# Hybrid SSD and forgetting-attention layer: the stores of the output weights' differences, issued by GpSimd instead of the load queue

## The chip, the cores and the metric

The kernel runs on one core of one Trainium2 chip. A core has five engines that run side by side, each with its own queue in order: TensorE (PE in the profile; PEld is its weight load), VectorE (DVE), ScalarE (ACT), GpSimd (POOL) and SyncE (SP), which here only issues DMAs. An engine whose next instruction must wait on a semaphore stops there, and all that stands behind it waits too. A DMA is issued by an engine (SP, ScalarE or GpSimd here) and then moves its bytes on the core's 16 DMA engines. The metric is the device time of one execution in microseconds (us).

## The reference

A decoder layer for 1024 positions of width 1024, in float32, with two branches beside each other:

```python
h    = _rmsnorm(x, pre_g)
proj = jnp.einsum('bld,de->ble', h, w_in)   # z_ssm xBC dt | q k v f | z_att g_ssm g_att
...                                          # xBC: causal convolution of 4 taps, silu
y    = _ssd_chunked(xs, dt, a, b_ssm, c_ssm, d_skip)      # 8 chunks of 128 positions, 16 heads of 64
y_ssm = grouped_rmsnorm(y * silu(z_ssm)) * ssm_norm_g
o     = _forgetting_attention(q, k, v, log_f)             # softmax(q k' / 8 + F[t] - F[s]), causal
y_att = o * silu(z_att)
p_ssm = jnp.einsum('ble,ed->bld', y_ssm, w_branch_ssm)
p_att = jnp.einsum('ble,ed->bld', y_att, w_branch_att)
merged = sigmoid(g_ssm) * p_ssm + sigmoid(g_att) * p_att
out   = jnp.einsum('bld,de->ble', merged, w_out)
x     = x + _rmsnorm(out, post_g)
```

(shortened: `grouped_rmsnorm` stands for the four groups' norm that the reference writes out). The part that the change touches prepares `w_out`, the 1024 x 1024 output weights, for the last product.

## The kernel before

**Products with fewer multiplications.** Every large product is done on 2 x 2 blocks with seven block products instead of eight (class `Pair`). The moving operand is a matrix of four blocks b11, b12, b21, b22; beside blocks themselves the seven products need four differences of them: t1 = b12 - b11, t2 = b22 - t1, t3 = t2 - b11, t4 = t2 - b21. Each block product is twelve matmuls of 512 columns into one PSUM bank: four steps of 128 rows, each with high and low parts of the operands (high x high, high x low, low x high), since a float32 value is split into a rounded part and its remainder. The stream of products (class `Stream`) advances by half steps of six matmuls, `Stream.half`.

**Stages.** The stream of projections runs from the start to the end. Beside it run, in turn: a prologue that normalises and transposes x; for four groups of heads the convolution, the chunked recurrence (`ssd`) and the gated norm; then attention for eight pairs of heads; last the two branch products, the merge and the output product. A generator of the other work yields how many half steps of the stream go between its own pieces.

**The output weights' differences.** In the last product the output weights are the moving operand; the object `ops_w` of class `Operands` (line 1182) stands for it. Its differences are made early, during the stage of the recurrence. `weights_work` (L1054) makes a list of chores, for 4 row blocks and 2 halves of 256 columns, eight pieces in all, and `Stream.half` takes one chore per half step (L1353 hands them over). The chores of one piece come from `differences` (L200) with `room` 4, which is the number of empty chores between a load and its use:

- load b12 into tile x (L230) and b11 into tile y (`fetch`, L209), both from SP;
- four empty chores; GpSimd subtracts t1 = x - y into x (L214); then `keep`: store t1 (L196) and load b22 into y;
- four empty chores; the low part of b22 by ScalarE and VectorE (L240, L241) and its store from SP (L248); GpSimd subtracts t2 = y - x into x; `keep`: store t2 and load b11 into y;
- four empty chores; t3 = x - y into y, `keep`: store t3; its low part (L243, L244) and store (L248); three empty chores; load b21 into y; four empty chores;
- t4 = x - y into x; `keep`: store t4; low part and its store.

Each x and y is a single tile of 128 x 256 float32, one pair for each half; the tile of the low part, `wl`, is a single one. The stores go to a DRAM copy and are read back for the last product, after 1100 us. So 32 subtractions, 32 stores of differences (L196), 24 stores of low parts (L248) and 40 loads.

**Order.** `pin` keeps an instruction in program order within its engine. The subtractions, the stores and the low parts' roundings are pinned, and `ops_w` is made with `order=pin`, which pins its loads, and `queue=nc.sync`, so that its stores go by SP. The other two operands, `ops_s` and `ops_a`, have the default queue, GpSimd. All that isn't pinned is ordered at build time by a planner with its own estimate of times, which also sets the semaphore waits.

**Neighbours on the queues.** In the same stage SP issues the projections' weight loads (`raw`, L348), the loads and stores of the recurrence (csb L861, z L996, ys L1051), and stores of q, k, v and z (L672, L688, L689, L845). GpSimd does three steps for each chunk of the recurrence: `xe` (L906) that feeds the state's product, `ce` (L913) that feeds the output's, and the decay of the state `new` (L927), to which VectorE adds the chunk's part (L931). The copy of a product out of PSUM on ScalarE is L412, the split of the stationary operand L355 (ScalarE) and L357 (VectorE), its sums L364 and L380.

## Time and profile before

| | |
|---|---|
| median of 3 runs | 1288.71 us (1287.9 to 1292.36) |
| profiled execution | 1288.07 us; span of its instructions 1286.4 us |
| granted TensorE clock, mean | 0.998 |
| busy in the span: TensorE, VectorE, ScalarE, GpSimd | 1248.9, 1016.0, 797.3, 288.5 us |
| DMA: moved, mean rate | 233.60 MB, 182 GB/s |
| queue of SP (q1), GpSimd (q0), ScalarE (q10): share of the DMA engines | 49.6%, 3.4%, 2.2% |

The span runs from the first to the last instruction of the profiled execution; its own time is 1.67 us longer. In the views, L196 is line 196 of the kernel; a `q` behind an engine's name is its sequencer, which waits, branches or issues; "idle before" is how long an engine did nothing before an instruction, and the arrow names whose semaphore ended that. `wd` is the name of both tiles x and y, `t_w` of the DRAM copies of the differences, `wl` of the low part's tile. A matmul's record is longer than the step from one matmul to the next, since they overlap.

### The profile page before, as it was taken

How to read it: one execution, taken by the hardware profiler on the slowest of the kernel's cores; microseconds unless marked ns; L12 is line 12 of the kernel's file. 1: busy time of each engine (PE TensorE's matmuls, PEld its weight loads, DVE VectorE, ACT ScalarE, POOL GpSimd, SP SyncE). 2: the span in 40 equal slices, each digit the busy share in tenths (PEclk: the TensorE clock that was granted, in tenths of full speed). 3: DMA queues.
4: the chain of work that ended last, by engine and by line, in shares of the span. 5: the costliest groups of instructions: out<-in, count | busy, mean ns of one | idle time of the engine just before them, and what ended most of it. 6: DMA issues, size and time to landing. Idle time of an engine off the chain costs nothing.

```text
span 1286.4 us, 21104 instructions
## 1 busy us (share of the span) xinstructions
PE 1248.9 (97%) x7066; PEld 986.9 (77%) x7066; DVE 1016.0 (79%) x1979; ACT 797.3 (62%) x1728; POOL 288.5 (22%) x307
## 2 busy tenths in 40 slices
PE   6999999999999999899999999999999999999998
PEld 4787888788887888778777777777777777678886
DVE  6998888798789888788677766766678877976976
ACT  8745666566556656566556666666667655753754
POOL 0000330024102320043001222222111222346052
PEclk9999999999999999999999999999999999999999
DMA  7333543545353454445475664666678657766933
GB/s 282 98 110 70 159 143 126 194 142 153 129 192 124 149 170 150 136 140 144 162 243 173 215 221 161 235 208 209 202 276 269 212 194 241 238 203 201 372 114 101
DMA packets 154669, 233.60 MB, mean 182 GB/s; under 512 B 17216, under 2 KB 62656, under 8 KB 154560
## 3 DMA queue, kind: packets, MB, share of 16 engines
q1 hardware_dynamic: 142016, 205.53, 49.6%
q0 software_dynamic: 6400, 16.10, 3.4%
q10 hardware_dynamic: 6144, 10.62, 2.2%
q8 instruction: 56, 0.92, 0.3%
q14 instruction: 53, 0.43, 0.1%
HBM read 162.99 MB, written 72.34 MB: 183 GB/s over the span
## 4 chain that ended last, share of the span: by engine, by line
PE 70%; DVE 11%; DMA 9%; ACT 5%; issue 4%; SPq 1%; POOL 1%; DVEq 0%; ACTq 0%
PE pb L130 30%; PE pc L130 17%; PE pd L130 5%; PE av L130 4%; PE pt L133 4%; PE s L130 4%; DVE wop L357 2%; PE yps L130 2%; DMA raw<-in_wu 2%; DMA q<-qh_dram 1%; PE tr L133 1%; PE st L130 1%; DMA xt<-in_x 1%; ACT wop L355 1%; DVE sum L364 1%
## 5 line engine op out<-in xcount | busy, mean ns | idle before, releaser
L357 DVE TENSOR_TENSOR wop<-sum,wop 128x512 fp32r<-128x512 f32 x174 | 138.1, 794 | 58.1 <-ACT wop L355 56.6
L355 ACT ACTIVATE wop<-sum 128x512 fp32r<-128x512 f32 x174 | 108.8, 626 | 99.0 <-DVE sum L364 45.1
L1563 ACT ACTIVATE ex<-ex,nm 128x512 f32<-128x512 f32 (+1 forms) x192 | 116.0, 605 | 55.4 <-DVE nm L1558 55.0
L412 ACT ACTIVATE s<-pb 128x512 f32<-128x512 f32 x141 | 83.6, 593 | 103.0 <-PE pb L130 89.1
L357 DVE TENSOR_TENSOR wop<-raw,wop 128x512 fp32r<-128x512 f32 x149 | 114.2, 768 | 37.0 <-ACT wop L355 36.9
L130 PE MATMUL pc<-x3h,wop 128*128 128x512 f32 x384 | 132.3, 401 | 2.6 <-ACT wop L355 2.0
L130 PE MATMUL pb<-x0h,wop 128*128 128x512 f32 x384 | 132.5, 401 | 0.1
L130 PE MATMUL pc<-x2h,wop 128*128 128x512 f32 x384 | 131.9, 400 | 0.3 <-DVE u L424 0.3
L130 PE MATMUL pb<-x5h,wop 128*128 128x512 f32 x376 | 127.9, 397 | 2.2 <-ACT s L412 2.2
L130 PE MATMUL pb<-x6h,wop 128*128 128x512 f32 x376 | 128.3, 397 | 1.3 <-ACT s L412 1.3
L130 PE MATMUL pb<-x4h,wop 128*128 128x512 f32 x376 | 127.6, 397 | 0.3 <-DVE wop L357 0.3
L1558 DVE CUSTOM_DVE_ANT_0 ex<-s,fb 128x512 f32<-128x512 f32 (+1 forms) x192 | 96.4, 551 | 12.7 <-PE s L130 12.7
L355 ACT ACTIVATE wop<-raw 128x512 fp32r<-128x512 f32 x151 | 94.0, 624 | 19.0 <-PE pc L130 11.3
L130 PE MATMUL pd<-x1h,wop 128*128 128x512 f32 x264 | 89.1, 395 | 0.0
L130 PEld LDWEIGHTS pc<-x3h,wop 128*128 128x128 f32 x384 | 72.8, 190 | 20.7 <-ACT wop L355 3.7
L130 PEld LDWEIGHTS pc<-x2h,wop 128*128 128x128 f32 x384 | 72.1, 188 | 17.1 <-issue 1.5
L130 PEld LDWEIGHTS pb<-x0h,wop 128*128 128x128 f32 x384 | 72.6, 189 | 16.4 <-issue 0.6
L130 PEld LDWEIGHTS pb<-x5h,wop 128*128 128x128 f32 x376 | 70.7, 188 | 18.4 <-ACT s L412 3.0
L130 PEld LDWEIGHTS pb<-x6h,wop 128*128 128x128 f32 x376 | 70.6, 188 | 16.9 <-ACT s L412 1.7
L130 PEld LDWEIGHTS pb<-x4h,wop 128*128 128x128 f32 x376 | 70.5, 188 | 16.2 <-DVE wop L357 0.9
L214 POOL TENSOR_TENSOR wd<-wd 128x256 f32<-128x256 f32 x32 | 30.4, 951 | 228.4 <-DMA wd<-in_wo 108.2
L130 PE MATMUL pc<-x3l,wop 128*128 128x512 f32 x192 | 75.7, 394 | 0.7 <-DVE x3l L282 0.7
(342 smaller groups left out, 3002.6 us busy)
## 6 DMA issues: line engine op xcount, KB each, us to landing
raw<-in_wu SPq DMA_DIRECT2D x128, 256.0 KB, 3.9
csb<-cs_dram SPq DMA_DIRECT2D x32, 256.0 KB, 5.5
fb<-f_dram SPq DMA_DIRECT2D x16, 512.0 KB, 6.2
wd<-in_wo SPq DMA_DIRECT2D x40, 128.0 KB, 3.3
rb<-st_dram SPq DMA_DIRECT2D x34, 128.0 KB, 3.2
xt<-in_x SPq DMA_DIRECT2D x8, 512.0 KB, 5.8
gs_dram<-th ACTq DMA_DIRECT2D x16, 256.0 KB, 3.6
qh_dram<-th SPq DMA_DIRECT2D x16, 256.0 KB, 4.2
```

What stands on the lines that cost most here:

```text
L130: return tc.keep_in_program_order(nc.tensor.matmul(*args, **kw))
L133: return tc.keep_in_program_order(nc.tensor.transpose(out_, in_, idn))
L214: pin(nc.gpsimd.tensor_tensor(t[out_], t[a_], t[b_], ALU.subtract))
L355: nc.scalar.activation(op[:, 0], src, AF.Copy, scale=sign)
L357: nc.vector.tensor_tensor(op[:, 1], src, op[:, 0], ALU.subtract)
L364: self.adds.tensor_tensor(t, x, y, ALU.add)
L412: nc.scalar.activation(s, ps, AF.Copy)
L1558: nc.vector.tensor_tensor_reduce(to, bank(u, e), fb[hp, h][:, e, 0 : w[u]], 1.0, 3.0e38, ALU.add, ALU.min, nm)
L1563: nc.scalar.activation(to, to, AF.Exp, scale=-1.0, bias=nm, accum_out=hd.at(hd.sm, i, h, e))
```

## The change

The method `store` of `Operands`, which writes a difference to DRAM, no longer issues its DMA from the queue that the object was made with but always from GpSimd. For `ops_s` and `ops_a` that is the same queue as before; for `ops_w` the 32 stores of 128 x 256 values move from SP's queue to GpSimd's. The stores of the low parts at L248 use the object's queue still, so they stay on SP.

```diff
         def store(self, name, j, t, cols=slice(0, HALF)):
-            pin(self.queue.dma_start(self.dram[name][j][:, cols], t))
+            pin(nc.gpsimd.dma_start(self.dram[name][j][:, cols], t))
             if cols.stop == HALF:
                 self.made.add((name, j))
```

On GpSimd the store takes the place in program order that it had: in the chore behind the subtraction's, with whatever GpSimd does for the recurrence in between.

## Prediction

> **What bounds the kernel now.** I read the page first, then the busy times by stretch, then the waits of TensorE, and only then the queue that the change touches.

> ```profile
> span 1286.4 us, 21104 instructions
> PE 1248.9 (97%) x7066; PEld 986.9 (77%) x7066; DVE 1016.0 (79%) x1979; ACT 797.3 (62%) x1728; POOL 288.5 (22%) x307
> 127.00:645.00 518.00, 511.60 (x2680) 412.96 (x2679) 429.58 (x715) 319.66 (x646) 115.78 (x112) 1.00 0.48 151
> ```

> The last row gives the length, the busy time of TensorE, its weight loads, VectorE, ScalarE and POOL, the granted clock and the DMA's share for the stretch from the first load of the output weights (127.9 us) to the last piece of their differences. TensorE is idle for 518.0 - 511.6 = 6.4 us in it. POOL works 115.8 us of 518, so it has room; SP's queue only matters through what it delivers late to others. Whatever the change takes off a queue can win no more than those 6.4 us and what they cause. TensorE's waits in the same stretch name their causes:

> ```profile
> PE pc L130 <- ACT wop L355: 2.0, 1, 2.0
> PE pb L130 <- ACT s L412: 1.3, 1, 1.3
> PE st L130 <- POOL xe L906: 1.2, 2, 0.9
> PE tr L133 <- DVE xs L813: 1.1, 1, 1.1
> ```

> There are few stalls and each is short. The sum below asks which of them the stores stand behind.

> **The change part by part.** It moves 32 stores of 128 KB (t1 to t4, eight pieces each). The 24 stores of low parts at L248 stay on SP, and so do the 40 loads.

> ```profile
> L209 SPq DMA_DIRECT2D wd<-in_wo x32: 333/423/737, 128.3 to 625.6; - x32
> L214 POOL TENSOR_TENSOR wd<-wd x32: 725/742/1954, 133.3 to 628.5; 128x256 f32<-128x256 f32 x32
> L196 SPq DMA_DIRECT2D t_w<-wd x32: 319/382/609, 135.2 to 638.0; - x32
> SPq L196 <- POOL wd L214: 25.1, 11, 4.2
> ```

> *Removed from SP:* 32 x 0.382 = 12.2 us of issuing, and 25.1 us in 11 waits for the subtraction, by these rows. Only part of the waiting goes. After t1 and t2 the very next entry is the load of the next block into y, and y is read by the same subtraction, so that load must wait for it just as the store did; the wait moves from L196 to L209. After t3 and t4 the next entry of that chain is the low part's store, which waits for VectorE's rounding that itself follows the subtraction; other transfers may slip in before it. So what surely remains is the issue time of one store, with its step to the next (0.42 us, from 525.30 to 525.72 in the chain below), by which the following load leaves earlier.

> *What those 0.42 us are worth.* The longest stall, 2.0 us, hangs on such a load. The chain of waits there:

> ```profile
> 524.03 1.25 POOL wd L214
> 525.30 0.33 SPq L196
> 525.72 3.27 DMA wd<-in_wo
> 529.07 0.04 ACT wl L240
> 529.40 0.58 ACT s L412
> 530.53 0.70 DVE wop L357
> 534.46 0.69 DVE sum L364
> 535.23 0.56 ACT wop L355
> 535.88 0.47 PE L130 MATMUL pc<-x3h,wop 128*128 128x512 f32 x1 [2.04 <-ACT wop L355]
> ```

> The subtraction ends at 525.28, SP issues the store, then the load of b22 at 525.72; it lands at 528.99, and ScalarE, which works in order, is stopped at the rounding L240 until then. Behind it stand the copy out of PSUM (L412) and the weights' split, then VectorE's queue, and TensorE starts 2.04 us late. Without the store the load leaves at about 525.30 and everything behind it moves up 0.42 us. That is **-0.4 us**.

> *The clock behind that stall.* Granted clock around this stall, and around the 1.3 us stall at 250.18:

> ```profile
> 537.00:540.00 3.00, 3.00 (x9) 2.32 (x8) 3.00 (x6) 2.31 (x8) 0.00 (x0) 0.50 0.51 157
> 248.00:252.00 4.00, 2.71 (x12) 1.90 (x12) 2.29 (x5) 1.42 (x3) 0.73 (x1) 1.00 0.77 250
> ```

> After 2.04 us of idle TensorE ran at half clock for some 3 us and 9 matmuls, so about 1.5 us were lost besides; after 1.3 us it did not. With the stall cut to 1.6 us it lies between the two, a little nearer to 1.3. A dip that stays is worth 0, one that goes 1.5 us; I take **-0.8** and keep both ends. [...]

> *Other loads on SP* behind one of the 32 stores also leave up to 0.4 us earlier, but TensorE's other stalls in the list are held by something else: the 1.3 us one by a b21 load that SP issued right behind a store waiting for VectorE, the 1.1 us one by VectorE's convolution. Bounds: 0 to the rest of the 6.4 us (4.4); value 0, as no row links them to a store.

> *Added on POOL.* The trace has no store of 128 KB from POOL; the nearest are those of the same line for the other operands, 256 KB.

> ```profile
> L196 POOL DMA_DIRECT2D t_s<-x x12: 547/577/600, 691.9 to 894.2; - x12
> 696.00 0.59 POOL L196 DMA_DIRECT2D t_s<-x  x1 [0.31 <-POOL x L214]
> DMA to landing us min/median/max: 2.4/5.0/6.8
> ```

> Each takes 0.58 us of POOL, and 0.31 us more where it stands directly behind its subtraction. So 32 x (0.58 to 0.89) = 18.6 to 28.5 us on an engine that is idle for 402 us of the stretch. Behind it on POOL stand the recurrence's own steps:

> ```profile
> 149.83 0.74 POOL L214 TENSOR_TENSOR wd<-wd 128x256 f32<-128x256 f32 x1
> 150.53 1.15 POOL L927 TENSOR_TENSOR new<-new,cdec 128x256 f32<-128x256 f32 x1
> 154.48 0.61 POOL L906 TENSOR_TENSOR xe<-xdt,tend 128x256 f32<-128x256 f32 x1 [2.80 <-DVE xdt L874]
> POOL xe L906 <- DVE xdt L874: 199.4, 28, 70.5
> 159.27 0.39 PE L130 MATMUL yps<-ce,new 128*64 128x128 f32 x4
> ```

> In the worst order the store sits between 149.83's subtraction and the state's decay `new`, which then starts 0.89 us later, at about 151.4. The state is read by the second `yps` after it, at 159.27, so some 7 us cover it. The next step, `xe`, waits for VectorE: all 28 do, (199.4 - 70.5) / 27 = 4.8 us each without the first, 2.80 us in this row, which swallows 0.89. Cost **0**; if the cover were gone, at most one store before each of the 28 steps, 28 x 0.89 = 24.9 us, is the upper bound. VectorE's addition behind `new` can be 0.9 us late in some places; VectorE is idle 88 us of the stretch.

> *The data's way.* The differences are read back only after 1100 us; the landing time plays no part there. Within a piece, t2 overwrites the tile that t1's store reads, so t2 waits for that landing: the second rival.

> **Sum.** 1288.07 us (this execution: span 1286.4 and 1.67 around it) - 0.4 - 0.8 + 0 = 1286.9. This execution was 0.64 us under the median of the runs (1288.71), so I forecast 1287.5 for the median, within 0.1% of before.

> **The rivals.**

> *SP was worth more.* Both waits at t3 and t4 and the earlier loads remove the 2.0 and 1.3 us stalls, the clock dip, and 1.2 to 2.5 us more. Time: 1288.7 - (2.0 + 1.3 + 1.5 + 1.2) = 1282.7. For it: 25.1 us of waiting at the head of the queue. Against: y ties the next load to the same subtraction.

> *The store's landing becomes the wait (slower).* Now t2 follows t1 closely where SP had fallen behind:

> ```profile
> 205.60 0.33 SPq L196 DMA_DIRECT2D t_w<-wd  x1
> 208.58 0.74 POOL L214 TENSOR_TENSOR wd<-wd 128x256 f32<-128x256 f32 x1 [3.01 <-DMA wd<-in_wo]
> ...
> 529.15 0.74 POOL L214 TENSOR_TENSOR wd<-wd 128x256 f32<-128x256 f32 x1 [3.88 <-DMA wd<-in_wo]
> t_w<-wd SPq DMA_DIRECT2D x32, 128.0 KB, 3.2
> ```

> From SP a store lands in 3.2 us. From POOL, with the 5.0 us of the 256 KB stores, issued at 205.9, it lands at 210.9 and t2 starts 2.3 us later (4.1 with 6.8). Four pieces look like this, the first and the last of them shown. If t3's rounding on ScalarE followed t2 at once, ScalarE would stop 2.3 us four times and TensorE with it: 1288.7 + 9.2 = 1297.9, and up to four clock dips of 1.5 us more. It decides only once the lateness exceeds the room between t2 and t3, which the program sets at six half steps of six matmuls, at least 6 x 6 x 0.227 = 8.2 us (0.227 us is TensorE's step, as from 528.41 to 528.64 in the timeline). 2.3 and 4.1 both stay below it.

> ```profile
> 528.41 0.39 PE L130 MATMUL pd<-x1l,wop 128*128 128x512 f32 x1
> 528.64 0.61 PE L130 MATMUL pd<-x1h,wop 128*128 128x512 f32 x2
> ```

> *POOL's stores stretch beside VectorE.* POOL's arithmetic does stretch here; beside it the busy times of the rest of the program:

> ```profile
> L906 POOL TENSOR_TENSOR xe<-xdt,tend x28: 612/614/3003, 132.7 to 593.8; 128x256 f32<-128x256 f32 x28
> ```

> ```profile
> 645.00:1287.00 642.00, 622.15 (x3850) 485.43 (x3848) 477.94 (x1057) 394.78 (x928) 171.53 (x187) 1.00 0.64 214
> ```

> If a store took 3.0 us as the longest `xe` did, 0.3 + 3.0 = 3.3 would exceed the 2.80 us before `xe` by 0.5; with a store before half of the 28 steps that is 7 us: 1295.7. Against it: the stores of the later stages took 547 to 600 ns while VectorE was busy 478 of 642 us, 74%, against 83% here. [...]

> *The planner orders the rest anew.* Only pinned instructions keep program order; others are ordered at build time by estimated times, which the move changes. The largest event seen costs 2.0 + 1.5 = 3.5 us, so one more or one fewer gives 1285.2 to 1292.2.

> *Nothing moves:* the wait simply passes to L209 and the 0.42 us are lost elsewhere: 1288.7.

> **How the numbers follow.** Forecast 0.55, SP worth more 0.12, landing 0.07, stretched stores 0.03, planner 0.16, nothing moves 0.07. A measurement of this kernel can tell about 0.5% from no change, 6.4 us: below 1282.3 or above 1295.2. Below: half of the first rival (0.06) and 0.02 of the planner's; above: 0.09 from landing, stretching and the planner's tail. The forecast's own range is 1286 to 1289 (dip gone or kept, and 0.5 of scatter); for 8 in 10 it reaches into the first rival and the planner's ends, 1283.5 to 1292.5.

> **What would show it.** Right: no L196 on SP; POOL's stores at 0.55 to 0.60 us and most behind their subtraction by 0.3; L209's waits for POOL growing by part of the 25.1 us; TensorE's idle time in the stretch 5 to 7 us; the stall at 535.88 at 1.6 us. Wrong: POOL stores of 1 us or more, `st` or `yps` waiting for POOL in many places, t2 waiting for the store's landing with ScalarE stopped at L243 behind it, or new stalls in the attention stage, which would be the planner's.

## The result, and the profile after

The changed kernel takes 1297.88 us (median of 6 runs, 1294.80 to 1301.76), against 1290.12 us for the kernel before beside it (6 runs, 1287.78 to 1292.36): ratio 1.0062, 95% interval [1.0044, 1.0080]. It is slower by 0.6%, outside the range that was forecast (1283.5 to 1292.5). Its profiled execution took 1296.72 us with a span of 1294.9 us, 8.5 us longer than that of before.

The page of the changed kernel, and the stretch of the output weights' pieces in the columns of the prediction (length, busy time of TensorE, its weight loads, VectorE, ScalarE and GpSimd, granted clock, DMA share, GB/s):

```profile
span 1294.9 us, 21110 instructions
PE 1248.9 (96%) x7066; PEld 986.5 (76%) x7066; DVE 1016.3 (78%) x1979; ACT 797.0 (62%) x1728; POOL 304.6 (24%) x339
127.00:645.00 518.00, 506.01 (x2657) 408.69 (x2655) 423.47 (x705) 316.51 (x642) 134.44 (x144) 1.00 0.48 148
```

TensorE has exactly the work of before, 1248.9 us. In the stretch its idle time rose from 6.4 to 518.0 - 506.0 = 12.0 us. Its waits there name the causes (us in total, times, longest):

```profile
PE yps L130 <- DVE m L884: 3.4, 2, 1.7
PE pb L130 <- ACT s L412: 2.7, 1, 2.7
PE tr L133 <- DVE xs L813: 2.1, 1, 2.1
PE pc L130 <- ACT wop L355: 1.4, 1, 1.4
PE pc L130 <- DVE u L424: 1.3, 2, 0.8
PE st L130 <- POOL xe L906: 0.9, 1, 0.9
```

The first line is new: before, `yps` waited for nobody. The second grew from 1.3 to 2.7 us, the fourth shrank from 2.0 to 1.4. The operations that were moved look as they were forecast; this is the group view of `wd`, and the waits of SP in the stretch:

```profile
L214 POOL TENSOR_TENSOR wd<-wd x32: 719/830/1930, 133.2 to 633.8; 128x256 f32<-128x256 f32 x32
L196 POOL DMA_DIRECT2D t_w<-wd x32: 557/559/762, 135.4 to 634.8; - x32
SPq L209 <- POOL wd L214: 7.7, 5, 2.5
```

A store costs GpSimd 0.56 us, SP has none left, and of its 25.1 us of waiting for the subtraction 7.7 us stayed, now at the loads.

Matching the two traces matmul by matmul shows where the 8.5 us arise. The stop near 250 us is 1.4 us longer, and half clock behind it costs 1.6 more. The two waits for `m`, near 291 and 431 us, add 1.7 and 1.9, two waits near 394 and 550 us 0.8 each. The stop that the prediction counted on, at 535.88, gives back 2.1 with its half clock. With small steps between that makes 5.7 us at 557 us; 2.8 more come behind 645 us, 1.6 of them in one place near 1113 us.

The orders of the two programs explain part of it. Engine by engine, compared by line and tile: SP, ScalarE, GpSimd and TensorE have the same order in both but for the 32 moved stores, VectorE has seven exchanges, that is, pairs of instructions whose order is turned round. So the planner did order anew, on one engine. What the seven exchanges cost and what the stores cost had to be parted by experiment.

### The profile page after: what moved, and what is told of

Its sections match the earlier page's. It is cut to its first block, busy times and chain, and to the rows that moved or that the text cites. A ratio compares the mean times of both kernels' runs of the same rounds, so it can differ in the third digit from the quotient of the medians.

```text
span 1294.9 us, 21110 instructions
## 1 busy us (share of the span) xinstructions
PE 1248.9 (96%) x7066; PEld 986.5 (76%) x7066; DVE 1016.3 (78%) x1979; ACT 797.0 (62%) x1728; POOL 304.6 (24%) x339
## 4 chain that ended last, share of the span: by engine, by line
PE 69%; DVE 11%; DMA 9%; ACT 5%; issue 4%; SPq 1%; POOL 0%; DVEq 0%; ACTq 0%; POOLq 0%
PE pb L130 31%; PE pc L130 16%; PE pd L130 5%; PE av L130 4%; PE pt L133 4%; PE s L130 4%; DVE wop L357 3%; PE yps L130 2%; DMA raw<-in_wu 2%; DMA wd<-in_wo 1%; PE tr L133 1%; DMA xt<-in_x 1%; DVE sum L364 1%; PE st L130 1%; DMA th<-gs_dram 1%
## 5 line engine op out<-in xcount | busy, mean ns | idle before, releaser
L357 DVE TENSOR_TENSOR wop<-sum,wop 128x512 fp32r<-128x512 f32 x174 | 138.5, 797 | 56.9 <-ACT wop L355 56.5
L355 ACT ACTIVATE wop<-sum 128x512 fp32r<-128x512 f32 x174 | 108.8, 626 | 99.0 <-DVE sum L364 45.4
L412 ACT ACTIVATE s<-pb 128x512 f32<-128x512 f32 x141 | 83.7, 594 | 105.6 <-PE pb L130 91.7
L357 DVE TENSOR_TENSOR wop<-raw,wop 128x512 fp32r<-128x512 f32 x149 | 115.8, 779 | 37.6 <-ACT wop L355 37.4
L130 PE MATMUL pc<-x3h,wop 128*128 128x512 f32 x384 | 131.2, 398 | 2.4 <-ACT wop L355 1.4
L130 PE MATMUL pc<-x2h,wop 128*128 128x512 f32 x384 | 132.0, 400 | 1.3 <-DVE u L424 1.3
L130 PE MATMUL pb<-x0h,wop 128*128 128x512 f32 x384 | 132.2, 400 | 0.4 <-ACT x0h L1253 0.3
L130 PE MATMUL pb<-x6h,wop 128*128 128x512 f32 x376 | 129.4, 400 | 2.7 <-ACT s L412 2.7
L130 PE MATMUL pb<-x5h,wop 128*128 128x512 f32 x376 | 128.0, 397 | 2.8 <-ACT s L412 2.8
L130 PE MATMUL pb<-x4h,wop 128*128 128x512 f32 x376 | 127.6, 397 | 0.3 <-DVE wop L357 0.3
L355 ACT ACTIVATE wop<-raw 128x512 fp32r<-128x512 f32 x151 | 94.0, 624 | 19.0 <-PE pc L130 11.3
L130 PE MATMUL pd<-x1h,wop 128*128 128x512 f32 x264 | 89.1, 395 | 0.0
L130 PEld LDWEIGHTS pc<-x3h,wop 128*128 128x128 f32 x384 | 72.1, 188 | 20.1 <-issue 2.8
L130 PEld LDWEIGHTS pc<-x2h,wop 128*128 128x128 f32 x384 | 72.2, 188 | 18.5 <-DVE u L424 2.2
L130 PEld LDWEIGHTS pb<-x6h,wop 128*128 128x128 f32 x376 | 71.3, 190 | 18.6 <-ACT s L412 3.2
L130 PEld LDWEIGHTS pb<-x0h,wop 128*128 128x128 f32 x384 | 72.6, 189 | 16.8 <-ACT x0h L1253 1.1
L130 PEld LDWEIGHTS pb<-x5h,wop 128*128 128x128 f32 x376 | 70.6, 188 | 19.4 <-ACT s L412 4.1
L130 PEld LDWEIGHTS pb<-x4h,wop 128*128 128x128 f32 x376 | 70.5, 188 | 16.0 <-issue 0.7
L214 POOL TENSOR_TENSOR wd<-wd 128x256 f32<-128x256 f32 x32 | 31.8, 994 | 213.9 <-DMA wd<-in_wo 161.5
L1465 POOL DMA_DIRECT2D st_dram<-st x48 | 27.3, 571 | 210.8 <-ACT st L1463 207.7
## 6 DMA issues: line engine op xcount, KB each, us to landing
wd<-in_wo SPq DMA_DIRECT2D x40, 128.0 KB, 3.0
rb<-st_dram SPq DMA_DIRECT2D x34, 128.0 KB, 3.1
```

The costliest lines, as they stand in the source:

```text
L130: return tc.keep_in_program_order(nc.tensor.matmul(*args, **kw))
L214: pin(nc.gpsimd.tensor_tensor(t[out_], t[a_], t[b_], ALU.subtract))
L355: nc.scalar.activation(op[:, 0], src, AF.Copy, scale=sign)
L357: nc.vector.tensor_tensor(op[:, 1], src, op[:, 0], ALU.subtract)
L412: nc.scalar.activation(s, ps, AF.Copy)
L1465: pin(nc.gpsimd.dma_start(st_dram[self.hp, n, :, 256 * h : 256 * h + 256], st[4 * h : 4 * h + 4, :]))
```

## The experiments

All ratios are to the kernel before, run beside them. The last column is the mean over all runs of the granted clock; what half clock costs is estimated as (1 - clock) x span: 3.6 us for before (0.9972), 5.8 for the changed kernel (0.9955).

| run | median us | ratio, 95% interval | clock |
|---|---|---|---|
| changed kernel | 1297.88 | 1.0062 [1.0044, 1.0080] | 0.9955 |
| e4, the same again | 1296.11 | 1.0049 [1.0032, 1.0066] | 0.9950 |
| e2, VectorE's new order alone | 1296.52 | 1.0044 [1.0027, 1.0062] | 0.9958 |
| e13, two of its exchanges alone | 1294.99 | 1.0040 [1.0025, 1.0056] | 0.9963 |
| e3, changed, these two undone | 1292.25 | 1.0015 [1.0001, 1.0030] | 0.9952 |
| e1, 32 stores on GpSimd, order of before | 1293.57 | 1.0022 [1.0004, 1.0039] | 0.9956 |
| e14, the same again | 1293.74 | 1.0034 [1.0021, 1.0046] | 0.9952 |
| e6, 31 stores | 1291.70 | 1.0006 [0.9992, 1.0020] | 0.9958 |
| e5, one store | 1290.46 | 1.0001 [0.9988, 1.0014] | 0.9970 |
| e9, the first 20 stores | 1288.60 | 0.9987 [0.9972, 1.0001] | 0.9968 |
| e10, the last 20 stores | 1288.24 | 0.9984 [0.9972, 0.9997] | 0.9978 |
| e7, early load of b21, stores on SP | 1289.89 | 0.9995 [0.9984, 1.0007] | 0.9968 |
| e8, the same, 32 stores on GpSimd | 1293.16 | 1.0024 [1.0013, 1.0035] | 0.9956 |
| e12, early load for the output weights alone | 1287.60 | 0.9979 [0.9962, 0.9997] | 0.9980 |
| e15, the same with the last 20 stores | 1285.25 | 0.9963 [0.9948, 0.9978] | 0.9985 |

e11 ran once, in 1292.76 us, and so has no ratio. Lines in these kernels lie up to 20 further on than in before, since names were added: m L884 is L900 or L902 there.

### The order and the stores, each alone

An ordering edge tells the planner which of two instructions of an engine comes first; it adds no wait. Numbers count each kind in program order.

```diff
+    def queue_behind(later, earlier):     # (kind, number): later stands behind earlier
+        tc.add_manual_dep(marks[later].ins, marks[earlier].ins.name, NoSync)
...
 # e1: changed kernel, every engine in the order of before
+    queue_behind(wop 40, new 1); queue_behind(z 7, new 6); queue_behind(z 11, new 12)
+    queue_behind(sum 33, m 10); queue_behind(sum 51, m 18)
+    queue_behind(xdt 11, sum 34); queue_behind(xdt 27, sum 70); queue_behind(xdt 3, sum 16)
 # e2: kernel before, VectorE in the order of the changed kernel
+    queue_behind(new 1, wop 40); queue_behind(new 6, z 7); queue_behind(new 12, z 11)
+    queue_behind(m 10, sum 33); queue_behind(m 18, sum 51)
+    queue_behind(sum 34, xdt 11); queue_behind(sum 70, xdt 27)
 # e3: changed kernel;  e13: kernel before, with the two the other way round
+    queue_behind(sum 33, m 10); queue_behind(sum 51, m 18)
```

(The expectation of e1 speaks of nine edges; there are eight.) e4 has no edit.

> The changed kernel with nine ordering edges, so that every engine's order of instructions is the one of before; what is left of the change is that GpSimd issues the 32 stores. Theory 'order' (all of the 7.8 us come from VectorE's new order): within 1.5 us of the kernel before, about 1290, and TensorE's waits for VectorE's m L884 (1.65 and 1.73 us) gone. Rival 'stores' (the two waits for m are the order's, 3.5 us, the rest is from the stores on GpSimd: the later landing of the b21 load at 243 us, its clock dip, the drift behind 645 us): 3 to 5 us slower than before, about 1294, with a stop of TensorE of 2.7 us near 250 and half clock behind it. The prediction's own sum (-0.4 and -0.8): 1 us faster than before.

> The kernel before, its stores still on SP, with seven ordering edges that give VectorE the order of the changed kernel; all other engines keep theirs. Theory 'order': as slow as the changed kernel, 6 to 9 us over before, about 1298, with two waits of TensorE's yps for m L884 near 290 and 431 us. Rival 'stores': only the two waits, 3.5 us over before, about 1293.6.

> The changed kernel with two edges only: the sums L364 that wait for a raw load go behind the decay product m L884 again, in the second chunk of groups 1 and 2; the other exchanges of VectorE's order stay. If the two waits cost what TensorE's idle time shows: 3.5 us faster than the changed kernel, about 1294.4. If the time goes elsewhere behind the two waits (given back later): under 1.5 us faster. If the clock or later stages hang on them as well: 6 us or more faster.

> The changed kernel once more, unaltered: a second profile. If the longer landing of the b21 load at 243 us (6.63 us) and the half clock at 253 us belong to the kernel, they are there again, with TensorE's stop of 2.7 us near 250; if they are chance of one execution, the stop is 1.3 us as before and the profile is some 2.8 us shorter. Time 1297.9 within 2 us.

> The kernel before, stores on SP, and two ordering edges alone: in the second chunk of groups 1 and 2 the sum L364 that waits for a raw load goes ahead of the decay product m L884. If the whole loss of VectorE's new order is these two: 4 to 6 us slower than before, ratio 1.003 to 1.0045, two waits of TensorE's yps for m L884 of 1.7 us or more. If the five other exchanges carry a part: ratio under 1.0025.

The order alone costs 0.44%, 5.7 us, with the stores still on SP: the larger part of the loss is not in the stores. Two of the seven exchanges carry nearly all of it, 0.40% or 5.2 us, and taking these two out of the changed kernel (e3) wins 1.0049 - 1.0015 = 0.34%, 4.4 us, between the 3.5 and the 6 us of its expectation. Here is the first of the two in VectorE's timeline, in the kernel before (start, length, in brackets idle before and releaser):

```profile
285.39 1.01 DVE L884 TENSOR_TENSOR m<-m,cbm 128x512 f32<-128x512 f32 x1
288.52 0.91 DVE L364 TENSOR_TENSOR sum<-raw 128x512 f32<-128x512 f32 x1 [2.12 <-DMA raw<-in_wu]
```

and in the changed kernel, with TensorE's row behind it:

```profile
290.89 0.69 DVE L364 TENSOR_TENSOR sum<-raw 128x512 f32<-128x512 f32 x1 [3.17 <-DMA raw<-in_wu]
291.50 1.25 DVE L884 TENSOR_TENSOR m<-m,cbm 128x512 f32<-128x512 f32 x1
...
292.90 0.44 PE L130 MATMUL yps<-m,xdt 128*64 128x128 f32 x4 [1.65 <-DVE m L884]
```

The sum waits for a load, and VectorE stands idle for it, 2.12 or 3.17 us in these rows. Behind `m` that costs TensorE nothing; ahead of `m` it holds up `m`, and `yps` with it. In e13, with these two exchanges alone, TensorE's waits show:

```profile
PE yps L130 <- DVE m L900: 5.5, 2, 2.8
```

The two were 1.65 and 1.73 us in the changed kernel's first profile, 2.35 and 2.25 in e4, 2.13 and 3.39 in e2, 2.65 and 2.83 in e13: the price hangs on when a load lands in that execution. (e4, the same kernel again, had the stop near 250 us again, 2.8 us, as expected, but no half clock behind it; half clock came at 431 and 550 us instead.)

The stores alone (e1) cost 0.22%, and 0.34% in e14, more than the 0.06 to 0.22% expected of it. e3, with the 32 stores and five of the exchanges, stands at only 0.15%, so the price of the stores is known to some 0.15 to 0.34%. 'Order' falls: e1 was to be within 1.5 us of before, and e2 lay under its 6 us. 'Stores' has the size of e1 about right, but e2 cost more than its 3.5 us, and the stores' price is not where it was looked for, as the next two groups show.

### One store, all but one

```diff
 # e5: e1, and
-            pin(nc.gpsimd.dma_start(self.dram[name][j][:, cols], t))
+            one = (name, j, cols.start) == ("t3", 0, 256)
+            queue = nc.gpsimd if one else self.queue
+            pin(queue.dma_start(self.dram[name][j][:, cols], t))
 # e6: the same with  queue = self.queue if one else nc.gpsimd
```

> Every engine in the order of before, and one of the 32 stores alone on GpSimd: t3 of the second piece, issued at 237 us. In the four profiles with all stores on GpSimd the load of csb that SP issues 3 to 4 us later took 7.3 to 7.5 us to land and with it all behind it, the b21 load too (6.6 to 6.8 us), and TensorE stopped 2.2 to 2.9 us near 250; in the two with all on SP 5.7 to 6.1, 5.0 to 5.2 and 1.1 to 1.3 us. Theory 'this store' (it alone lengthens these landings): b21 lands in 6.6 us or more and the stop near 250 is over 2.2 us. Rival 'all that is shifted' (SP's queue as a whole, or the DMA engines' backlog): 5.2 us and 1.3 us as before. Time in both cases within 2 us of before.

> The opposite: every engine in the order of before, 31 stores on GpSimd, the t3 store of the second piece on SP. Theory 'this store': b21 lands in about 5.2 us, the stop near 250 is 1.1 to 1.3 us, and the time is about 2.5 us under that of all 32 on GpSimd in this order, at 1290 to 1291. Rival 'all that is shifted': 6.6 us, a stop over 2.2 us, and 1293.

e5 has a stop of 1.0 us near 250, e6 one of 2.5, with the csb load landing in 5.9 and 7.2 us. So not this store. "All that is shifted" didn't hold either: with the first 20 stores on GpSimd (e9), the six ahead of this place among them, the stop was 1.5 us, where e9's expectation had 2.2 or more; with the first 12 on SP and the last 20 on GpSimd (e10) it was 2.4. Over the profiles with the b21 load in its old place the csb load that SP issues near 241 us lands either in 5.7 to 6.1 us, with a stop of 1.0 to 1.6, or in 7.0 to 7.5 us, with a stop of 2.2 to 2.9. For e9 the trace gives no landing of it; the stop of 1.5 puts e9 with the early ones. This is the view of that load in before, e10 and the changed kernel:

```profile
DMA to landing us min/median/max: 6.1/6.1/6.1
```

```profile
DMA to landing us min/median/max: 7.1/7.1/7.1
```

```profile
DMA to landing us min/median/max: 7.3/7.3/7.3
```

All six profiles with 31 or 32 stores on GpSimd and the b21 load in its old place were late, none of the four with one store or none, and one of three between, counting e9 by its stop. What makes the load late stays open; the number of stores on GpSimd ahead of it does not decide it, since e9 and e11 have the same six there as the six late ones, and e10 has none.

### The 129th DMA of GpSimd

These six profiles, and that of e8, have something else in common, near 1100 us, 460 us behind the last moved store. In the changed kernel, GpSimd, then SP, ScalarE and TensorE:

```profile
1101.26 0.59 POOL L1465 DMA_DIRECT2D st_dram<-st  x1 [3.38 <-ACT st L1463]
1104.72 0.58 POOL L1465 DMA_DIRECT2D st_dram<-st  x1 [2.87 <-issue]
1105.30 0.59 POOL L1654 DMA_DIRECT2D ya_dram<-zr  x1
...
1106.44 1.09 SPq L1471 DMA_DIRECT2D rb<-st_dram  x2
1107.69 0.47 SPq L266 DMA_DIRECT2D x1l<-ya_dram  x1
...
1111.70 0.63 ACT L281 ACTIVATE x1h<-x1l 128x512 fp32r<-128x512 f32 x1 [4.39 <-DMA x1l<-ya_dram]
...
1113.09 0.33 PE L133 MATMUL pt<-ident,ex 128*128 128x128 f32 x1 [1.47 <-ACT ex L1563]
```

"issue" is time in which the engine waited for nothing that the profile shows: GpSimd stands still for 2.87 us between two stores, which in the kernel before follow each other at once. The two stores issued from 1104.72 us on are late, SP's loads wait for them, ScalarE is stopped for 4.39 us at L281 (2.83 in before), and TensorE for 1.47 us, where it did not stop before. GpSimd's DMAs up to 1101.5 us, in groups (busy us and mean ns behind the bar):

```profile
L1465 POOL DMA_DIRECT2D st_dram<-st x43 | 24.4, 570 | 203.7 <-ACT st L1463 203.7
L196 POOL DMA_DIRECT2D t_w<-wd x32 | 18.4, 575 | 7.8 <-POOL wd L214 7.8
L1654 POOL DMA_DIRECT2D ya_dram<-zr x13 | 7.5, 581 | 0.8 <-DVE zr L1503 0.8
L196 POOL DMA_DIRECT2D t_s<-x x12 | 6.9, 574 | 2.7 <-POOL x L214 2.7
L1104 POOL DMA_DIRECT2D ms_dram<-th x12 | 6.6, 549 | 78.5 <-DVE th L1103 68.2 <-DMA x4l<-t_a 10.3
L196 POOL DMA_DIRECT2D t_a<-y x7 | 3.9, 552 | 0.0
L196 POOL DMA_DIRECT2D t_a<-x x5 | 2.9, 580 | 0.6 <-POOL x L1672 0.6
L196 POOL DMA_DIRECT2D t_s<-th x4 | 2.3, 582 | 0.3 <-POOL th L214 0.3
```

43 + 32 + 13 + 12 + 12 + 7 + 5 + 4 = 128. The kernel before issues 108 DMAs from GpSimd in all, the changed one 140; the standstill stands ahead of the 129th. Three runs test the count, all in the order of before:

```diff
-            pin(nc.gpsimd.dma_start(self.dram[name][j][:, cols], t))
+            self.stored = getattr(self, "stored", 0) + 1
+            queue = nc.gpsimd if self.stored <= 20 else self.queue      # e9
+            queue = nc.gpsimd if self.stored > 12 else self.queue       # e10
+            queue = nc.gpsimd if self.stored <= 26 else self.queue      # e11
+            pin(queue.dma_start(self.dram[name][j][:, cols], t))
```

> Every engine in the order of before; the first 20 stores on GpSimd, the last 12 on SP. In the six profiles with 31 or 32 stores on GpSimd it stood still for 2.85 to 2.89 us with nothing that released it, each time ahead of its 129th DMA, at 1098 to 1105 us (GpSimd's DMAs: 139 or 140 there, 108 before); behind it TensorE's pt waited 1.2 to 1.9 us for ScalarE. With 20 stores GpSimd issues exactly 128. Theory 'the 129th DMA': no such standstill, and pt starts near 1106 without a wait over 0.5 us; the stop near 250 (2.2 us or more) stays, since its six stores are as before; 1 to 2 us under all 32, about 1292. Rival (code or place, not count): the standstill is there at the same place.

> Every engine in the order of before; the first 12 stores on SP, the last 20 on GpSimd, again 128 DMAs of GpSimd. If the whole price of the stores on GpSimd is the stop near 250 us (from the six stores ahead of it) and the 129th DMA, with the half clock behind either: stop near 250 of 1.1 to 1.3 us, no standstill of GpSimd, time within 1 us of the kernel before, clock as before. If the price is spread over all stores: 1.5 us over before, by 20/32 of the 2.5.

> As the first 20, but 26 stores on GpSimd, 134 DMAs of it in all. Theory 'the 129th DMA': the standstill of 2.9 us moves six DMAs on, to the second of the two stores of st near 1120 us, and none is at the earlier place. Rival (a place in the code): it stays near 1100.

> All 32 stores on GpSimd, every engine in the order of before, once more: a standstill of GpSimd of 2.9 us ahead of its 129th DMA near 1101 us and a wait of pt for ScalarE of 1.2 us or more behind it. Ratio 1.0006 to 1.0022 as the two runs with 32 and 31 stores had it, some 3 us over the ones with 20.

e9 and e10 issue exactly 128 and have no standstill. In e11, with 134, it moved six DMAs on, as expected; GpSimd's timeline there:

```profile
1094.47 1.17 POOL L1483 DMA_DIRECT2D st_dram<-st  x2 [3.38 <-ACT st L1481]
...
1115.07 0.59 POOL L1483 DMA_DIRECT2D st_dram<-st  x1 [1.72 <-ACT st L1481]
1118.53 0.58 POOL L1483 DMA_DIRECT2D st_dram<-st  x1 [2.88 <-issue]
```

Over all kernels: every profile with more than 128 DMAs of GpSimd has it, eight of eight, 2.85 to 2.89 us long and each time ahead of the 129th; of the nine with up to 128 none has one. Why 128 is the number no trace shows, nor whether it counts DMAs or something that goes with them.

With 20 stores the kernel is faster than before, by 0.13 and 0.16% (the interval of the first just takes in no change); with 32 slower by 0.22 and 0.34%. The difference, 0.28 - (-0.15) = 0.43%, is 5.5 us; with 31 stores (1.0006) it would be 2.7. The 12 stores more and the 129th DMA lie in it together, and the eight profiles that have it show 1.2 to 1.9 us of stop behind the standstill, six of them with half clock behind that, by an estimate 1.7 us or more; none of the nine others has half clock at this place. Matched matmul by matmul, e14 lies 0.5 us behind the kernel before at 645 us, 2.6 at 1090 and 4.6 at 1120 us: in that execution the stores cost next to nothing in their own stretch, and 2.1 us arise in several places behind it. The standstill is shown; its share of those 2.7 to 5.5 us is only bounded.

e9 was expected at about 1292 us and came out at 1288.60. The expectation for e10, within 1 us of before, was missed by a little (0.16% is 2.1 us faster), and its "stop near 250 of 1.1 to 1.3 us" was wrong (2.4).

### The load of b21 earlier, and a version that beats both

```diff
 # e7 (stores on SP) and e8 (32 on GpSimd, with the edges of e1)
-            yield from (less("t3", "y", "x", "y"), keep(), *low("t3"), *wait[1:], lambda: fetch("b21"), *wait)
+            yield from (less("t3", "y", "x", "y"), keep(), *low("t3"), None, lambda: fetch("b21"), *wait, None, None)
 # e12: in the output weights' pieces alone; e15: e12 with the last 20 stores on GpSimd, with the edges
+            early = 2 if third else 0
+            yield from (less("t3", "y", "x", "y"), keep(), *low("t3"), *wait[1 + early:], lambda: fetch("b21"), *wait)
+            yield from (None,) * early
```

> The kernel before, stores on SP, with the load of b21 two chores earlier in each piece (one empty chore behind the low part's store and six ahead of the subtraction, in place of three and four); the planner orders the rest anew. If ScalarE's wait for this load near 250 us is the stall, the 1.1 to 1.3 us stop there goes: 1 us faster, 2 to 3 if half clock behind it went too. If the new order opens waits of its own, as the moved stores did: 3 us or more slower.

> The same earlier load of b21 with all 32 stores on GpSimd, and the nine ordering edges. Theory 'the stores' cost goes through the b21 load near 250 us': with the load early there is no stop of TensorE over 1.5 us near 250, and the time is that of the earlier load with stores on SP within 1 us. Rival 'the cost is spread': 2 us or more over it, with the granted clock 0.001 to 0.002 lower.

> The kernel before, stores on SP, the load of b21 two chores earlier in the output weights' pieces alone; the earlier run with this edit had changed the other two operands' chores as well, and with them the planner's order in attention, where it lost what it had won. Here all behind 645 us keeps the order of before. If the stops near 250 (1.1 to 1.3 us) and 536 us (2.0, and half clock behind it) go as in that run: 3 to 4.5 us faster than before, about 1286.5. If the time is given back at a later wait whatever the order: within 1 us.

> The early load of b21 of e12 and the last 20 stores on GpSimd (128 DMAs of it). If the two gains are at different stops they add: 0.9965. If both take away the same stop near 536 us and its half clock, as their traces say: no more than the better of them, 0.998.

The edit of e7 also lengthened the chores of the other two operands by two, and the planner changed its order in attention: the stops near 250 and 536 were gone and the kernel 5.2 us ahead at 535 us, then a longer wait near 541 us and a new one near 938, with half clock, took most of it: the time is that of before (0.9995). e8 stood 0.29% over e7 with a clock lower by 0.0012, the rival's case: it has the 129th DMA, and its stop near 250 was still 1.9 us.

e12 keeps the order behind 645 us (VectorE, ScalarE and SP differ from before in places up to 556 us) and is faster by 0.21%, 2.7 us, less than the 3 to 4.5 expected. With the 20 stores (e15) it is 0.37%, 4.8 us, faster than before and 0.9 to 1.0% faster than the changed kernel. So the two gains add, although e12 alone had already no stop near 536 us; where the second one arises no trace shows, and VectorE's order differs between e12 and e15 in a few places. The span of e15, its stretch, and its one long wait there:

```profile
span 1284.9 us, 21099 instructions
127.00:645.00 518.00, 513.57 (x2691) 415.43 (x2691) 432.72 (x717) 320.82 (x649) 128.74 (x134) 1.00 0.48 152
PE tr L133 <- DVE xs L832: 2.1, 1, 2.1
```

TensorE is idle for 4.4 us of the stretch, against 6.4 in before and 12.0 in the changed kernel. The span of this one profile says less than the six runs: 1282.40 to 1286.56 us.

## Why the prediction was wrong

**The gain on SP: the earlier start was right, what it was to win was not.** The term was -0.4 for the earlier load of b22 and -0.8 for the half clock behind it. The load did leave earlier: with the store on GpSimd it is issued 0.03 us behind the subtraction, with the store on SP 0.45 us. The step that failed is that everything behind it moves up by as much. Of six profiles with the store on GpSimd, a subtraction of 1.1 to 1.3 us and the b21 load in its old place, four (e1, e3, e11, e14) had the load land in 3.9 to 4.0 us, where those with the store on SP took 3.2 to 3.4, and TensorE's stop stayed at 2.04 to 2.06 us. In e14, against 525.72 and 529.07 in the chain of the prediction:

```profile
525.23 0.34 SPq L222 DMA_DIRECT2D wd<-in_wo  x1
529.22 0.42 ACT L253 ACTIVATE wl<-wd 128x256 fp32r<-128x256 f32 x1 [3.18 <-DMA wd<-in_wo]
```

In the other two, the changed kernel and e6, it landed in 2.5 and 2.7 us and the stop was 1.4 and 1.5, without half clock directly behind it in the changed kernel; why the landing differs no trace shows. And something else decides whether there is a stop at all. At 524 us two operations start within 0.05 us of each other, GpSimd's subtraction t1 and VectorE's sum. In the kernel before the subtraction took 1.24 us (the chain of the prediction) and the sum 0.69:

```profile
523.99 0.69 DVE L364 TENSOR_TENSOR sum<-sum,raw 128x512 f32<-128x512 f32 x1
```

In e9 it was the other way round:

```profile
523.78 0.73 POOL L229 TENSOR_TENSOR wd<-wd 128x256 f32<-128x256 f32 x1 [13.50 <-DVE sum L379]
...
523.81 1.25 DVE L379 TENSOR_TENSOR sum<-sum,raw 128x512 f32<-128x512 f32 x1
...
527.27 0.42 ACT L255 ACTIVATE wl<-wd 128x256 fp32r<-128x256 f32 x1 [0.75 <-DMA wd<-in_wo]
```

The load of b22 then leaves at 524.96 and not at 525.72, 0.5 us of it from the shorter subtraction, ScalarE waits 0.75 us for it and not 2.94, and TensorE does not stop for `wop` at all. The moved stores have no part in this: in e9 the store at this place is still SP's. Over the kernels with the b21 load in its old place t1 took 0.72 or 0.73 us three times (e4, e9, e10), each without this stop, and 1.13 to 1.30 ten times, each with one of 1.4 to 2.1 us; the changed kernel gave both, 1.4 in its first profile and none in e4. In five profiles with the two starts 0.01 to 0.04 us apart the one that came first was the short one: in before, e5 and e11 the sum starts ahead and takes 0.69 us, the subtraction 1.24 to 1.29; in e9 and e10 the subtraction starts ahead and takes 0.73 and 0.72 us, the sum 1.25 and 1.26. What ties the two lengths together no trace shows.

Much of what is won there is given back. In these three the next stop, for `tr`, lasts 2.4 to 2.7 us, against 1.1 in before; in e9, with half clock behind it:

```profile
542.61 0.33 PE L133 MATMUL tr<-ident,xs 128*128 128x128 f32 x1 [2.73 <-DVE xs L830]
```

e9's lead over the kernel before is 3.4 us at 541 us and nothing at 645 us. With 20 stores on GpSimd the kernel is faster by 0.13 to 0.16%, 1.7 to 2.1 us, but where these arise is not shown, and that this is the forecast's own gain is not shown either.

**"Cost 0" on GpSimd: failed.** The issue times were right (0.56 us, 0.30 behind the subtraction), and their cover held: `st` waited for `xe` 0.9 us in all, against 1.2 before. The step failed because it counted the stores' issue times in the stretch and not what GpSimd issues in the whole execution. The upper bound, 24.9 us, was made of issue times in the same stretch; a cost came 460 us later, as a standstill of 2.87 us ahead of the 129th DMA, 1.2 to 1.9 us of it felt by TensorE and half clock behind it in six profiles of eight, and no rival had it. The 108 DMAs of GpSimd could have been counted in the trace and 32 added, but no trace of before shows that 128 matters.

**The planner: the rival that mostly came true, at the wrong price.** It got a chance of 0.16 and 3.5 us, one event of stop and half clock. The order cost 5.2 to 5.7 us (e13, e2): two events in one build, each a product put behind an addition that waits for a load. The step "one more or one fewer" was the mistake: the planner turned seven pairs round, the same harmful pair in two groups of heads, and the price of each is the lateness of a load, 1.7 to 3.4 us, not the length of a stop already seen.

**The sum as it should have been:** -1.9 (20 stores on GpSimd) + 2.7 to 5.5 (12 more of them and the 129th DMA) + 5.2 to 5.7 (order) = 6.0 to 9.3 us; measured 8.0 and 6.3 (1.0062 and 1.0049). The terms are ratios between runs, none is worked out from the trace of before.

**The rivals that fell.** The store's landing: t2 did wait for it, as here, but it started no later than before (208.58), and ScalarE did not stop behind it. That this rival's time, 1297.9, is the measured one is chance.

```profile
207.76 1.23 POOL L214 TENSOR_TENSOR wd<-wd 128x256 f32<-128x256 f32 x1 [1.87 <-DMA t_w<-wd]
```

Stretched stores: 557 to 762 ns, never 3 us. "SP was worth more" and "nothing moves" are not what happened either, though with 20 stores, without the new order and the 129th DMA, the kernel came out between the forecast and the former.

**The signs named in advance.** No L196 on SP, 0.56 us a store, the waits moved to L209 in part: all seen, and all beside the point. The signs for the planner were put into attention; its work was in the stretch itself, as `yps` waiting for VectorE.

## What to carry to other kernels

Moving an instruction in a program whose order a planner makes is two changes, and the second can be the larger: compare the orders of the two programs first, engine by engine, and hold the old order with edges before pricing the move. Look in the new order for an operation with a load behind it that was put ahead of one that TensorE needs. Before adding DMAs to GpSimd's queue count all it issues in the execution: here 20 more were a small gain and 32 a loss, with part of the price paid far from the place of the edit.

## What the runs showed of the hardware

**Half clock came on a grid of 3.413 us in all 17 profiles.** In before it came behind a stop of 2.04 us; in e2 none came behind one of 3.39 us. The windows around both (columns as above), before, then e2, with TensorE's row in e2:

```profile
533.36:536.77 3.41, 1.37 (x7) 0.84 (x6) 3.41 (x7) 1.54 (x3) 0.00 (x0) 1.00 0.00 0
536.77:540.18 3.41, 3.41 (x10) 2.63 (x9) 3.41 (x6) 2.72 (x8) 0.00 (x0) 0.50 0.50 155
```

```profile
426.17:429.58 3.41, 1.69 (x8) 1.05 (x6) 0.00 (x0) 2.61 (x7) 1.34 (x2) 1.00 0.76 219
429.58:433.00 3.42, 1.75 (x23) 1.61 (x24) 3.15 (x6) 0.00 (x0) 0.00 (x0) 1.00 0.44 132
433.00:436.41 3.41, 3.41 (x19) 2.85 (x18) 1.91 (x4) 1.40 (x4) 2.14 (x3) 1.00 0.59 194
...
431.25 0.44 PE L130 MATMUL yps<-m,xdt 128*64 128x128 f32 x4 [3.39 <-DVE m L900]
```

**GpSimd's 129th DMA** stood behind 2.85 to 2.89 us in which the engine did nothing, in each of the eight profiles that have one.
